# Sums, low halves and splits of two inner norms and an output projection on one engine, with the norms' partition sums moved in the matmul order

## The chip, the cores and the metric

The kernel runs on one core of one Trainium2 chip. The core has five engines that run side by side, each working through its own instructions in order: TensorE (PE, matrix products), VectorE (DVE), ScalarE (ACT), GpSimd (POOL) and SyncE (SP, which here issues transfers). The metric is the device time of one execution in microseconds (us). Before the change the median of 3 runs is 2609.95 us (2608.35 to 2614.61).

## The reference

The program computes one layer of a hybrid decoder for a prompt of 1024 tokens and 8 single tokens of other sequences (the sample group), 1032 tokens in all, with model width 1024 and float32 throughout:

```python
x = layer_norm(ALPHA * x + 0.5 * swiglu(x, ffn1_w1, ffn1_w3, ffn1_w2), ln1_g, ln1_b)
m, st = hybrid_mixer(x, h0, rc0, S0, gc0, w_in, b_in, ...)
x = layer_norm(ALPHA * x + m, ln2_g, ln2_b)
x = layer_norm(ALPHA * x + 0.5 * swiglu(x, ffn2_w1, ffn2_w3, ffn2_w2), ln3_g, ln3_b)
```

swiglu(x, w1, w3, w2) is (silu(x w1) * (x w3)) w2 with an inner width of 2816. layer_norm takes the mean of each token over its 1024 values, subtracts it, takes the mean of the squares, multiplies by the reciprocal root of that, then by a weight, and adds a bias. The mixer projects x (w_in), runs a gated linear recurrence and a gated delta rule with 8 heads, gates and adds both, and multiplies the merged result by w_o.

## The kernel before

**Layout.** Activations lie with the model width on the 128 partitions, as 8 blocks (KD = 8), and the tokens along the row, in 3 chunks of 344 (TC). ACC holds the running values. TensorE takes its operands in a reduced form (fp32r), so every float32 value that goes into a product is split: a high half (h, a copy made by ScalarE) and a low half (l, value minus high half, made by DVE or POOL). `split` (L87) makes both, and `mm3_steps` (L124, matmul at L132) makes each product of three: h with xh, h with xl, l with xh. For the activations the halves are XH and XL; for weights wh and wl; for the last group of the down projections both are called w2h; for the merged input of the output projection their buffers bear names such as m_pre, m_lt, m_ga. A weight block comes as wraw (128 x 512) by a transfer of SyncE and is split in the same manner. `tt` (L91) is a two-operand operation on DVE or, if told so, on POOL, and `stt` (L94) one of DVE with two operations in one. In the profile they bear these two lines, wherever they are called from.

**Norms.** The class `LN` is a norm of one chunk in four steps. `add` adds the blocks of the chunk up as they are finished (tile s, from the tag s1; POOL for all but the last block). The first step of `finish` multiplies this sum by a matrix of ones on TensorE (L176; this is the sum of values over the partitions, and its mean is mu), subtracts the mean from the 8 blocks (DVE), squares them (ScalarE, tile lnq), and adds the squares in two partial sums, one on DVE and one on POOL. The second step is again a product with ones at L176, the sum of squares, then logarithm and exponential on ScalarE (tile rs) for the reciprocal root. The third applies it: a DVE operation with weight and root (ACC<-ACC,LNT,mu), bias and high half on ScalarE (XH), low half (XL) on DVE for blocks 0, 2, 4, 6 and on POOL for blocks 1, 3, 5, 7 (ON_POOL). Norm 2 also writes its output to the DRAM tile X2 from POOL's queue.

Norm 1 follows the first feed-forward, norm 2 the mixer, norm 3 the second feed-forward (4 chunks of 258 tokens, the last, the tail, by a way of its own).

**Who calls the steps.** `last_steps` (L507) runs the units of the projection ahead of a norm (one block of output for one chunk, 24 matmuls for the output projection, 12 for the last group of a down projection), and puts the norm of chunk t between the units of chunk t+1: its first step after unit 0, the second and third after unit LN_STEP = 4 (5 for norm 3). The norm of the last chunk is handed on to the next stage, as `fin`: `kqv_first` (L685) for norm 1, and the start of the second feed-forward (`plain`, L361) for norm 2.

**What sets the order.** The code writes down the order of issue, but a scheduler of the framework then orders each engine's instructions, except where a pin keeps them in program order. Within an engine, the order so made is kept. The output projection (w_o; `msplit` L1119, `unit` L1125) runs while the last head of the delta rule and the sample group's branch (`sample`, L1180) finish; `sample` yields to the main stream `wait(n)` times n between its small products, so a higher n puts its next product later among the matmuls.

Of the kernel before, what the change touches and what calls it, by code (L numbers as in the profile page):

```python
# [44 lines left out]
LAST = 0.97  # L45
LN_STEP = 4
WO_RATE = 2.53
SIDE = 2
ON_POOL = (1, 3, 5, 7)

# [6 lines left out]
def _build(ctx, tc, A):  # L57
# [97 lines left out]
    class LN:  # L155
# [5 lines left out]
        def add(self, m):  # L161
            y = ACC[:, m, self.s]
            self.order.append(m)
            self.ys.append(y)
            n = len(self.ys)
            if n == 2:
                self.s1 = third("s1", self.w)
                tt(self.s1, self.ys[0], y, OP.add, G)
            elif 2 < n < (KD - 1 if self.tail else KD):
                tt(self.s1, self.s1, y, OP.add, G)  # L170
            elif n == KD and not self.tail:
                tt(self.s1, self.s1, y, OP.add, V)

# [4 lines left out]
        def finish(self):  # L178
# [10 lines left out]
            for k in (0, 1, 3, 2, 4, 6, 5, 7) if self.tail else range(KD):  # L189
                y = ys[k]  # L190
                if not self.tail:
                    tt(y, y, mu, OP.subtract)
                elif k in (2, 5):
                    tt(y, y, mu, OP.subtract, G)
                else:
                    stt(y, pm, -1.0 / D, y, OP.mult, OP.add)
                q[k] = third("s2" if k < 2 else "s1" if self.tail and k > 5 else "lnq", w)
                act(q[k], y, AF.Square)
                if self.tail:
                    if k in (1, 2, 6, 7):  # L200
                        tt(q[k], q[k], q[{1: 0, 2: 3, 6: 4, 7: 5}[k]], OP.add)
                        parts.append(q[k])
                elif k > 1:
                    tt(q[k % 2], q[k % 2], q[k], OP.add, (V, G)[k % 2])
            if not self.tail:
# [4 lines left out]
            self.total(pv, parts)  # L210
            rs = third("mu", w)
            act(rs, pv, AF.Ln, scale=1.0 / D, bias=EPS)
            exps.append(act(rs, rs, AF.Exp, scale=-0.5))
            yield
            for i, (k, y) in enumerate(zip(self.order, self.ys)):
# [11 lines left out]
                h, l = XH[:, k, self.s], XL[:, k, self.s]  # L227
                if i in ON_POOL or self.gi == 2:
                    act(y, y, AF.Identity, bias=b_)
                    split(h, l, y, G if i in ON_POOL else V)  # L230
                    if self.gi == 2:
                        G.dma_start(X2[:, k, self.s], y)
                    continue
# [113 lines left out]
    def ffn(n, lnidx, out=None, side=None, fin=None):  # L347
# [16 lines left out]
        def plain(f, put, after=None, w=None, chunks=range(NT), raws=None):  # L364
            a1, a3 = w or weights(f, raws=raws)
            for t in chunks:
                s = ts(t)
                if n == 1 and f == 0 and t:
                    x_load(t)
                    x_split(t)  # L370
                p1 = psum("mm")
                mm3(p1[:, :TC], a1, xsl(t), KD)
                if fin and f == 0 and t < 2:
                    for _ in range(1 + t):
                        next(fin)
                p3 = psum("g")
                mm3(p3[:, :TC], a3, xsl(t), KD)
                put(s, p1[:, :TC], p3[:, :TC])
                if after:
                    after(t)  # L380
                if n == 1:
                    next(extra, None)
# [45 lines left out]
        with pool("ffnb%d" % n) as up:  # L428
# [26 lines left out]
            for gi, fs in enumerate(GROUPS):  # L455
# [25 lines left out]
                else:  # L481
# [6 lines left out]
                    def last(m, t, s, i):  # L488
                        if t == 0:
                            held[m] = w2load(m, eng=(V, G)[m % 2], hold=hold if n == 2 or m < 6 else None)  # L490
                        unit(m, t, s, held[m])
# [15 lines left out]
    def last_steps(lnidx, unit, chunks, order, out=None):  # L507
        fin = None
        for t, s in enumerate(chunks):
            tail = out is not None and t == len(chunks) - 1  # L510
            ln = LN(lnidx, s, out, tail)
            for i, m in enumerate(order[t]):
                yield from unit(m, t, s, i) or ()
                ln.add(m)
                if fin and i == 0:
                    next(fin)
                if fin and i == LN_STEP + (out is not None):
                    next(fin)
# [10 lines left out]
    def mixer(mc):  # L529
# [74 lines left out]
        with pool("mix") as mp:  # L604
# [80 lines left out]
            def kqv_first():  # L685
# [16 lines left out]
                next(fin)  # L702
                kq(0, 1)
                kq(1, 0)
                next(fin)
                next(fin)
                kq(1, 1)
                kq(0, 2)
                kq(1, 2)
# [408 lines left out]
            def msplit(t):  # L1118
# [3 lines left out]
                for k in range(KD):  # L1122
                    h, l = MHL[t][2 * k:2 * k + 2]
                    split(h[:, :n], l[:, :n], ACC[:, k, t * TC:t * TC + n], (V, G)[k % 2])

# [3 lines left out]
            def unit(m, t, s, i):  # L1129
                ms = MHL[t]  # L1130
                if i > 1 or t == 0:
                    if len(recent) == 2:
                        recent.pop(next(iter(recent)))
                    recent[m] = wload(A["w_o"][m], KD, eng=(V, G)[m % 2])
                p = psum("mm" if (m + t) % 2 else "g")
# [48 lines left out]
    def sample(c, up, tk, ta, blk, half):  # L1184
# [40 lines left out]
        nc.scalar.dma_start(A["conv_new"], SPX)  # L1225
        yield from wait(12)
        pn = psum("sq")
# [5 lines left out]
        V.tensor_scalar(DG, IDT, rn[:, 1:], None, op0=OP.mult)  # L1233
        yield from wait(6)
        nc.scalar.dma_start(A["s_h"], H0)
# [10 lines left out]
        V.tensor_copy(KE[:, 0], K_)  # L1246
        yield from wait(6)
        pq = psum("sq")
# [25 lines left out]
        tt(M, OS, OS, OP.mult)  # L1274
        yield from wait(8)
        pn = psum("sq")
# [9 lines left out]
        nc.scalar.dma_start(RTD, rt)  # L1286
        yield from wait(6)
        pn = psum("sq")
# [131 lines left out]
```

## Time and profile before

| | us |
|---|---|
| median of 3 runs (2608.35 to 2614.61) | 2609.95 |
| the profiled execution's own time | 2612.26 |
| its span | 2610.5 |
| busy TensorE (PE) | 2532.2 (97%) |
| busy DVE | 1742.9 (67%) |
| busy ScalarE (ACT) | 1134.0 (43%) |
| busy POOL | 467.4 (18%) |

The profile is of one execution, taken on the chip; its granted clock of TensorE is 0.986 of full speed in the mean. A row of a group reads: line, engine, operation, output tile<-input tiles, count | busy us and mean ns of one | idle time of the engine before it, and what ended that. A row of the waits reads: engine, what waited, then the engine and tile that it waited for: us in total, times, longest. A row of a timeline starts with start and duration in us. Shares of busy time are means over the whole span.

### The profile page before, as it was taken

The numbers are of one execution on the slowest core, as the hardware profiler recorded it, in microseconds if no ns is written. First come the engines' busy times: TensorE is split into PE (matmuls) and PEld (weight loads), VectorE is DVE, ScalarE is ACT, GpSimd is POOL, SyncE is SP. The second block draws the span as 40 slices with busy tenths as digits, with TensorE's granted clock in tenths as the row PEclk, the third lists the DMA queues.
The fourth block names the chain that finished last, engine by engine and source line by source line (L and its number), as shares of the span: only waits on it lengthen the run. The fifth ranks groups of instructions, "written<-read, shape, count | busy, mean of one in ns | idle before, by whom it ended". The sixth has DMA issues, their size and how long they took to land.

```text
span 2610.5 us, 47260 instructions
## 1 busy us (share of the span) xinstructions
PE 2532.2 (97%) x18374; PEld 2485.7 (95%) x18374; DVE 1742.9 (67%) x3641; ACT 1134.0 (43%) x2426; POOL 467.4 (18%) x633
## 2 busy tenths in 40 slices
PE   9999999999999999999999999998799999999996
PEld 8999999999888999999999999988799999999996
DVE  7666665644696676777767686777766666656446
ACT  5323333221463736565564637635533333332125
POOL 2000000300432112111112121134521111121013
PEclk9999999999998999999999999999899999999998
DMA  6222222432101111111111111124453444333221
GB/s 228 82 76 83 79 79 75 116 98 86 46 30 47 36 49 45 38 50 36 54 37 53 34 57 37 47 89 132 124 154 102 120 123 111 102 117 111 82 69 66
DMA packets 151135, 208.65 MB, mean 80 GB/s; under 512 B 35632, under 2 KB 76080, under 8 KB 150912
## 3 DMA queue, kind: packets, MB, share of 16 engines
q1 hardware_dynamic: 126176, 156.24, 19.6%
q0 software_dynamic: 13904, 43.34, 6.0%
q10 hardware_dynamic: 10832, 6.07, 0.8%
q8 instruction: 144, 2.36, 0.4%
q14 instruction: 79, 0.65, 0.1%
HBM read 164.60 MB, written 40.99 MB: 79 GB/s over the span
## 4 chain that ended last, share of the span: by engine, by line
PE 83%; ACT 6%; DVE 6%; DMA 1%; issue 1%; POOL 1%; ACTq 0%; SPq 0%; DVEq 0%; POOLq 0%
PE ps_mm L132 34%; PE ps_g L132 13%; PE ps_g L298 10%; PE ps_mm L298 10%; PE ps_sq L298 8%; PE ps_g L892 2%; ACT L88 2%; DVE ACC L94 2%; PE ps_sq L778 2%; ACT lnq L88 1%; PE ps_g L778 1%; PE ps_g L784 1%; DVE ACC L91 1%; POOL s L91 1%; DVE wl L91 1%
## 5 line engine op out<-in xcount | busy, mean ns | idle before, releaser
L132 PE MATMUL ps_mm<-XH,wh 128*128 128x344 f32 x1656 | 558.3, 337 | 6.1 <-ACT wh L88 5.8
L132 PE MATMUL ps_mm<-XH,wl 128*128 128x344 f32 x1656 | 532.9, 322 | 0.0
L132 PE MATMUL ps_mm<-XL,wh 128*128 128x344 f32 x1656 | 532.6, 322 | 0.1
L88 ACT ACTIVATE wh<-wraw 128x512 fp32r<-128x512 f32 (+2 forms) x360 | 213.9, 598 | 408.8 <-PE ps_mm L132 140.9
L132 PEld LDWEIGHTS ps_mm<-XH,wh 128*128 128x128 f32 x1656 | 314.4, 190 | 9.6 <-ACT wh L88 5.8
L132 PEld LDWEIGHTS ps_mm<-XL,wh 128*128 128x128 f32 x1656 | 314.4, 190 | 1.8 <-DVE XL L91 0.6
L132 PEld LDWEIGHTS ps_mm<-XH,wl 128*128 128x128 f32 x1656 | 313.8, 190 | 0.4 <-DVE wl L91 0.2
L91 DVE TENSOR_TENSOR wl<-wraw,wh 128x512 fp32r<-128x512 f32 (+3 forms) x339 | 232.3, 688 | 42.5 <-ACT wh L88 38.4
L298 PE MATMUL ps_g<-CH,wh 128*128 128x258 f32 x740 | 209.0, 282 | 0.0
L298 PE MATMUL ps_g<-CH,wl 128*128 128x258 f32 x740 | 208.9, 282 | 0.0
L298 PE MATMUL ps_g<-CL,wh 128*128 128x258 f32 x740 | 208.7, 282 | 0.0
L88 ACT ACTIVATE wh<-S 128x512 fp32r<-128x512 f32 x148 | 93.4, 631 | 197.9 <-PE ps_sq L298 126.8
L298 PE MATMUL ps_mm<-XH,wh 128*128 128x258 f32 x592 | 167.2, 282 | 0.0
L298 PE MATMUL ps_mm<-XH,wl 128*128 128x258 f32 x592 | 166.9, 282 | 0.0
L298 PE MATMUL ps_mm<-XL,wh 128*128 128x258 f32 x592 | 166.8, 282 | 0.0
L353 POOL DMA_DIRECT2D gs<-G x74 | 40.5, 547 | 652.1 <-DVE G L91 604.2
L91 DVE TENSOR_TENSOR wl<-S,wh 128x512 fp32r<-128x512 f32 x148 | 102.3, 691 | 70.9 <-ACT wh L88 70.6
L88 ACT ACT_TABLE_LOAD x109 | 139.8, 1283 | 5.4 <-issue 2.6
L132 PE MATMUL ps_g<-gl,wh 128*128 128x344 f32 x444 | 142.2, 320 | 0.0
L132 PE MATMUL ps_mm<-gl,wh 128*128 128x344 f32 x444 | 142.0, 320 | 0.0
L132 PE MATMUL ps_g<-gh,wh 128*128 128x344 f32 x444 | 142.0, 320 | 0.0
L132 PE MATMUL ps_mm<-gh,wh 128*128 128x344 f32 x444 | 142.0, 320 | 0.0
(536 smaller groups left out, 6884.9 us busy)
## 6 DMA issues: line engine op xcount, KB each, us to landing
wraw<-w SPq DMA_DIRECT2D x164, 256.0 KB, 2.8
wraw<-w_in SPq DMA_DIRECT2D x128, 256.0 KB, 2.6
gr<-gs SPq DMA_DIRECT2D x84, 258.0 KB, 2.8
wr<-w SPq DMA_DIRECT2D x76, 256.0 KB, 2.6
gs<-G POOLq DMA_DIRECT2D x74, 258.0 KB, 2.6
wraw<-w_o SPq DMA_DIRECT2D x40, 256.0 KB, 2.8
x<-ACC POOLq DMA_DIRECT2D x24, 172.0 KB, 2.2
y<-ACC SPq DMA_DIRECT2D x32, 129.0 KB, 1.9
```

Of the source, the lines that this page charges most:

```text
L88: return S.activation(out, in_, f, **kw)
L91: return (eng or V).tensor_tensor(out, a, b, op=op)
L94: return V.scalar_tensor_tensor(out, a, s, b, op0=op0, op1=op1)
L132: PE.matmul(p, a, b, start=(n == 0), stop=(n == 3 * nk - 1))
L298: PE.matmul(ps_[c], a[:, k, :], b, start=(start and n == 0), stop=(n == 11), skip_group_check=not start)
L353: G.dma_start(gs[f][:, s], x)
L778: x = PE.matmul(ck(p, i), a, b, start=True, stop=True)
L784: x = PE.transpose(ck(p, i), a, IDT)
L892: pin(PE.matmul(o[r, c, :], a(c), b(c), start=True, stop=True))
```

## The change

1. The running sums of values (`LN.add`) and both partial sums of squares run on DVE. The tail of norm 3 keeps the two subtractions and the two products on POOL that it has now.
2. The low halves XL of norms 1 and 2 are all made on DVE, with one form of code for all blocks: norm 1's blocks 1, 3, 5, 7 also lose an extra pass of ScalarE (Identity). The transfers to X2 stay on POOL's queue. The tile rs comes from the tag s1, and no longer from mu.
3. The low halves of the last group of the down projections (w2h), of w_o (wl) and of the merged input (m_...) are all made on DVE.
4. The steps of the norms move: in `last_steps` the first step stands after unit 1 instead of 0, second and third after unit 6 instead of 4 (5 for norm 3). For the last chunk of norm 1, `kq(0, 2)` stands ahead of the second step. For that of norm 2 the second and third step come in the second weight group's first chunk and no longer in the first group's second. The waits of `sample` become 16, 14, 14, 16 and 14.

```diff
-LN_STEP = 4
+LN_STEP = 6
-ON_POOL = (1, 3, 5, 7)
...
             if n == 2:
                 self.s1 = third("s1", self.w)
-                tt(self.s1, self.ys[0], y, OP.add, G)
-            elif 2 < n < (KD - 1 if self.tail else KD):
-                tt(self.s1, self.s1, y, OP.add, G)
-            elif n == KD and not self.tail:
-                tt(self.s1, self.s1, y, OP.add, V)
+                tt(self.s1, self.ys[0], y, OP.add)
+            elif 2 < n < (KD - 1 if self.tail else KD + 1):
+                tt(self.s1, self.s1, y, OP.add)
...
                 elif k > 1:
-                    tt(q[k % 2], q[k % 2], q[k], OP.add, (V, G)[k % 2])
+                    tt(q[k % 2], q[k % 2], q[k], OP.add)
...
-            rs = third("mu", w)
+            rs = third("mu" if self.tail else "s1", w)
...
-                if i in ON_POOL or self.gi == 2:
+                if self.gi == 2:
                     act(y, y, AF.Identity, bias=b_)
-                    split(h, l, y, G if i in ON_POOL else V)
-                    if self.gi == 2:
-                        G.dma_start(X2[:, k, self.s], y)
+                    split(h, l, y)
+                    G.dma_start(X2[:, k, self.s], y)
                     continue
...
-                if fin and f == 0 and t < 2:
-                    for _ in range(1 + t):
+                if fin and t == 0 and f < 2:
+                    for _ in range(1 + f):
                         next(fin)
...
-                            held[m] = w2load(m, eng=(V, G)[m % 2], hold=hold if n == 2 or m < 6 else None)
+                            held[m] = w2load(m, hold=hold if n == 2 or m < 6 else None)
...
-                if fin and i == 0:
+                if fin and i == 1:
                     next(fin)
-                if fin and i == LN_STEP + (out is not None):
+                if fin and i == LN_STEP:
...
                 kq(0, 1)
+                kq(0, 2)
                 kq(1, 0)
                 next(fin)
                 next(fin)
                 kq(1, 1)
-                kq(0, 2)
...
-                    split(h[:, :n], l[:, :n], ACC[:, k, t * TC:t * TC + n], (V, G)[k % 2])
+                    split(h[:, :n], l[:, :n], ACC[:, k, t * TC:t * TC + n])
...
-                    recent[m] = wload(A["w_o"][m], KD, eng=(V, G)[m % 2])
+                    recent[m] = wload(A["w_o"][m], KD)
...
-        yield from wait(12)
+        yield from wait(16)
...
-        yield from wait(6)
+        yield from wait(14)
...
-        yield from wait(6)
+        yield from wait(14)
...
-        yield from wait(8)
+        yield from wait(16)
...
-        yield from wait(6)
+        yield from wait(14)
```

The instructions of the engines then stand in another order. Three places show it. The code after the change is 4 lines shorter: L176 is L173 in it, L132 is L131, L91 is L90 and L94 is L93.

The first is TensorE in the output projection, first of before, around the sample group's product with ones (L1238, tile St); the other rows are products of the merged input (m_...) of two blocks.

```order
L132 MATMUL ps_mm<-m_hLT,wh 128x344
L132 MATMUL ps_mm<-m_lt,wl 128x344
L132 MATMUL ps_g<-m_pre,wh 128x344 x2
L132 MATMUL ps_g<-m_pre,wl 128x344
L1238 MATMUL ps_sq<-St,ONES 128x128
L132 MATMUL ps_g<-m_pre,wh 128x344 x2
L132 MATMUL ps_g<-m_pre,wl 128x344
L132 MATMUL ps_g<-m_rR,wh 128x344
```

The same engine and place, of the kernel with the change.

```order
L131 MATMUL ps_mm<-m_v,wh 128x344 x2
L131 MATMUL ps_mm<-m_v,wl 128x344
L1234 MATMUL ps_sq<-St,ONES 128x128
L131 MATMUL ps_mm<-m_lt,wh 128x344 x2
L131 MATMUL ps_mm<-m_lt,wl 128x344
L131 MATMUL ps_mm<-m_lt,wh 128x344
```

St stood a few matmuls into a block (behind the second pair of its first operands, m_pre); it now stands late in the next block, behind its products of m_v. Between it and the sample group's product before it (L1228, now L1224, tile at), from which its chain starts, there are now 42 matmuls of the projection instead of 18.

The second place is TensorE at the start of the second feed-forward, around the sum of squares of chunk 2 of norm 2, first of before (tile s_20892; ps_mm and ps_g are the two accumulators, XH and XL the operands of the chunk).

```order
L132 MATMUL ps_mm<-XH,wh 128x344
L132 MATMUL ps_mm<-XL,wh 128x344
L132 MATMUL ps_mm<-XH,wl 128x344
L176 MATMUL ps_sq<-s_20892,ONES 128x344
L132 MATMUL ps_g<-XH,wh 128x344
```

And of the kernel with the change (tile s_20880; w1wr is a weight of the second group).

```order
L131 MATMUL ps_mm<-XL,w1wr 128x344
L131 MATMUL ps_mm<-XH,w1wr 128x344
L173 MATMUL ps_sq<-s_20880,ONES 128x344
L131 MATMUL ps_g<-XH,w1wr 128x344
L131 MATMUL ps_g<-XL,w1wr 128x344
```

It stood among the products of the first weight group and now stands among those of the second.

The third place is DVE in the first feed-forward's last group, at the squares of chunk 0 of norm 1, first of before (s_7806 and s_7809 are the two partial sums of squares; POOL adds the squares to s_7809).

```order
L91 TENSOR_TENSOR ACC<-ACC,mu 128x344 x5
L91 TENSOR_TENSOR s_7806<-s_7806,lnq 128x344
L91 TENSOR_TENSOR ACC<-ACC,mu 128x344 x2
L94 SCALAR_TENSOR_TENSOR ACC<-ps_g,ACC 128x344
L91 TENSOR_TENSOR s_7806<-s_7806,lnq 128x344
L94 SCALAR_TENSOR_TENSOR ACC<-ps_mm,ACC 128x344
L91 TENSOR_TENSOR s_7806<-s_7806,s_7809 128x344
L94 SCALAR_TENSOR_TENSOR ACC<-ps_g,ACC 128x344
```

And with the change (s_7822 and s_7825 are the partial sums, s_7814 the sum of values of chunk 1).

```order
L90 TENSOR_TENSOR ACC<-ACC,mu 128x344 x3
L90 TENSOR_TENSOR s_7825<-s_7825,lnq 128x344
L90 TENSOR_TENSOR s_7822<-s_7822,lnq 128x344
L90 TENSOR_TENSOR s_7825<-s_7825,lnq 128x344
L93 SCALAR_TENSOR_TENSOR ACC<-ps_mm,ACC 128x344
L90 TENSOR_TENSOR s_7822<-s_7822,s_7825 128x344
L90 TENSOR_TENSOR s_7814<-s_7814,ACC 128x344
L93 SCALAR_TENSOR_TENSOR ACC<-ps_g,ACC 128x344
```

Both partial sums and the next chunk's sum of values now stand in DVE's own order, and POOL's order has none of them.

## The prediction

> **What bounds the kernel now.** I read the page first, for its engine shares and its chain.
>
> ```profile
> PE 2532.2 (97%) x18374; PEld 2485.7 (95%) x18374; DVE 1742.9 (67%) x3641; ACT 1134.0 (43%) x2426; POOL 467.4 (18%) x633
> ...
> PE 83%; ACT 6%; DVE 6%; DMA 1%; issue 1%; POOL 1%; ACTq 0%; SPq 0%; DVEq 0%; POOLq 0%
> ...
> L88 ACT ACT_TABLE_LOAD x109 | 139.8, 1283 | 5.4 <-issue 2.6
> ```
>
> TensorE (PE) is busy for 2532.2 of the 2610.5 us of the span and carries 83% of the chain (the last row, ScalarE's table loads at 1.28 us, is used further down). The change takes no matmul away, so all it can win is in the 2610.5 - 2532.2 = 78.3 us in which TensorE stands, and in what a lowered clock adds to its busy time. The next view is the list of TensorE's waits; its columns are the total, the number of waits and the longest, in us.
>
> ```profile
> PE ps_sq L176 <- DVE s L91: 28.7, 12, 7.6
> ...
> PE ps_g L132 <- DVE wl L91: 4.8, 3, 4.1
> PE ps_sq L1238 <- DVE St L1233: 4.3, 1, 4.3
> ...
> PE ps_sq L1277 <- DVE kt L91: 1.9, 1, 1.9
> PE ps_mm L132 <- POOL wl L91: 1.9, 2, 1.6
> PE ps_mm L132 <- DVE m_lt L91: 1.6, 1, 1.6
> ```
>
> These six rows hold 43.2 us, over half of the idle time. The first is the norms: their partition sums (L176) stand in TensorE's order before the vector engine (DVE) has their input. The view of line L176, asked for each norm's stretch by itself (660 to 760, 1770 to 1900, 2530 to 2611 us), divides it.
>
> ```profile
>   DVE s L91: 7.6, 4
> ```
> ```profile
>   DVE s L91: 10.9, 3
> ```
> ```profile
>   DVE s L91: 10.2, 5
> ```
>
> So norm 1 has 7.6 us, norm 2 10.9 and norm 3 10.2. Then the table by stretch: the two ends, length and busy PE, PEld, DVE, ACT and POOL, then the granted clock (PEclk).
>
> ```profile
> 660.00:760.00 100.00, 88.63 (x518) 82.48 (x517) 82.17 (x139) 57.52 (x105) 47.43 (x47) 0.97 0.13 38
> 1700.00:1760.00 60.00, 54.39 (x338) 51.61 (x337) 41.83 (x87) 21.53 (x55) 23.87 (x23) 0.94 0.28 88
> 1810.00:1860.00 50.00, 38.05 (x196) 35.14 (x195) 40.76 (x59) 25.96 (x53) 33.27 (x37) 0.86 0.35 116
> 1860.00:1900.00 40.00, 32.22 (x182) 30.98 (x181) 23.70 (x42) 24.03 (x44) 21.48 (x27) 0.87 0.47 136
> 2560.00:2600.00 40.00, 30.35 (x192) 27.70 (x190) 28.25 (x70) 25.05 (x54) 13.93 (x19) 0.88 0.22 73
> ```
>
> The second norm and the output projection (1700 to 1900) are worst: in 1810 to 1860 TensorE works 38.05 of 50 us, at a clock of 0.86, while DVE is busy for 40.76. A mean of 67% hides that. The timeline of TensorE shows what a long wait costs besides itself (start, duration, idle time before it in brackets).
>
> ```profile
> 743.34 1.13 PE L176 MATMUL ps_sq<-s,ONES 128*128 128x344 f32 x2 [2.46 <-DVE s L91]
> ...
> 744.55 0.49 PE L132 MATMUL ps_mm<-XL,wh 128*128 128x344 f32 x1
> 744.84 0.49 PE L132 MATMUL ps_mm<-XH,wl 128*128 128x344 f32 x1
> ...
> 1746.57 0.48 PE L132 MATMUL ps_g<-m_pre,wh 128*128 128x344 f32 x2
> 1746.89 0.32 PE L132 MATMUL ps_g<-m_pre,wl 128*128 128x344 f32 x1
> 1751.47 0.80 PE L1238 MATMUL ps_sq<-St,ONES 128*128 128x128 f32 x2 [4.26 <-DVE St L1233]
> ...
> 1752.63 0.49 PE L132 MATMUL ps_g<-m_pre,wl 128*128 128x344 f32 x1
> 1752.92 0.49 PE L132 MATMUL ps_g<-m_rR,wh 128*128 128x344 f32 x1
> ...
> 1881.13 1.51 PE L176 MATMUL ps_sq<-s,ONES 128*128 128x344 f32 x2 [7.59 <-DVE s L91]
> ```
>
> Two matmuls start within 0.32 us before the wait of 4.26 (0.16 us each) and 0.29 us apart behind it. Each matmul at that pace loses 0.13 us, and some 17 of them 2.2 us. The row at 743.34 shows the same 0.29 us behind a gap of only 2.46 us. [...] I go by the row and charge any wait over 2.4 us about 2 us more.
>
> **Why DVE is late.** Two timelines, DVE's and then POOL's (GpSimd's), around 1841 and 1873 us.
>
> ```profile
> 1841.01 3.78 DVE L94 SCALAR_TENSOR_TENSOR ACC<-ACC,LNT,mu 128x344 f32<-128x344 f32 x1
> ...
> 1872.04 0.69 DVE L91 TENSOR_TENSOR w1S<-wraw,w1wr 128x512 fp32r<-128x512 f32 x1 [5.44 <-ACT w1wr L88]
> 1872.65 2.22 DVE L91 TENSOR_TENSOR ACC<-ACC,mu 128x344 f32<-128x344 f32 x5
> ```
> ```profile
> 1841.35 0.94 POOL L91 TENSOR_TENSOR XL<-ACC,XH 128x344 fp32r<-128x344 f32 x1
> 1842.23 0.94 POOL L91 TENSOR_TENSOR s<-s,ACC 128x344 f32<-128x344 f32 x1
> 1843.11 1.30 POOL L91 TENSOR_TENSOR wl<-wraw,wh 128x512 fp32r<-128x512 f32 x1
> ...
> 1875.05 5.45 POOL L91 TENSOR_TENSOR s<-s,lnq 128x344 f32<-128x344 f32 x3 [10.59 <-ACT lnq L88]
> ```
>
> Undisturbed, five DVE operations of 128x344 take 2.22 us, 0.44 each (one alone I take at 0.50, an estimate, since the ends of neighbours overlap), and one of 128x512 0.69. The one at 1841.01 took 3.78 us, while three POOL operations ran back to back from 1841.35 to 1844.41. It ended at 1844.79, behind the last of them. DVE's operation appears to have stood for all three. How far that holds on the whole is seen in the groups, kept apart by form, of 1690 to 1900 us (busy us, mean ns), of DVE and of POOL.
>
> ```profile
> L91 DVE TENSOR_TENSOR wl<-wraw,wh 128x512 fp32r<-128x512 f32 x26 | 23.7, 914 | 5.6 <-ACT wh L88 5.6
> L94 DVE SCALAR_TENSOR_TENSOR ACC<-ACC,LNT,mu 128x344 f32<-128x344 f32 x24 | 20.1, 886 | 3.8 <-ACT mu L88 3.8
> L91 DVE TENSOR_TENSOR ACC<-ACC,XL 128x344 f32<-128x344 f32 x24 | 16.8, 702 | 0.2
> ```
> ```profile
> L91 POOL TENSOR_TENSOR wl<-wraw,wh 128x512 fp32r<-128x512 f32 x20 | 27.6, 1384 | 11.1 <-ACT wh L88 9.2 <-ACT r L88 1.9
> L91 POOL TENSOR_TENSOR s<-s,ACC 128x344 f32<-128x344 f32 x15 | 15.0, 997 | 27.0 <-DVE ACC L91 18.3 <-DVE m_pre L91 3.5 <-PE ps_mm L132 3.5
> ...
> L91 POOL TENSOR_TENSOR s<-s,lnq 128x344 f32<-128x344 f32 x9 | 12.6, 1404 | 22.9 <-ACT lnq L88 22.5
> L91 POOL TENSOR_TENSOR XL<-ACC,XH 128x344 fp32r<-128x344 f32 x12 | 12.2, 1013 | 0.2
> ```
>
> **The change part by part.**
>
> *Moving work to DVE, norm 2 and output projection.* It takes over 20 weight splits, 20 x 0.69 = 13.8 us, and 15 + 9 + 12 small ones from the POOL rows, with 3 first sums and about 12 merged-input splits from the diff: 51 x 0.44 = 22.4. Together 36 us. What it gets back, if POOL no longer holds it: wl 26 x (0.914 - 0.69) = 5.8, LNT 24 x (0.886 - 0.50) = 9.3, the third row 24 x 0.20 = 4.8, together 19.9, and more from the groups not shown. Net, DVE has some 0 to 16 us more in a stretch of 210; it was not full in the mean, though it was locally. What POOL took 1.0 to 1.4 us for arrives after 0.44 to 0.69.
>
> *Norm 1.* The diff moves 18 sums, 9 adds of squares and 12 low halves (39 x 0.44 = 17.2) and 4 weight splits (2.8): 20 us on a DVE that is busy 82.17 of 100. The refund by the same rule lies between 0 and all of it.
>
> *Norm 3.* 23 sums, 9 adds, 4 splits: about 32 x 0.42 + 2.8 = 16 us, beside 28.25 of 40 busy; it fits. ScalarE loses 12 Identity passes in norm 1. I cost that at nothing, because ScalarE is at 57.52 of 100 there.
>
> *The later partition sums*, from the order of TensorE's instructions, at 0.16 us a matmul of 344 columns and about 0.12 at 258 (an estimate: 0.16 x 258/344). In norm 2 the sum of squares of chunk 1 stands 119 matmuls behind the sum of values instead of 41, 12.5 us later; that of chunk 2 80 instead of 49, 5 us later. The 10.9 us of that row are the 7.59 and 3.3 more. The 3.3 go. Of 7.59, 5.0 are covered by the shift, and the three POOL adds that took 5.45 us become three of 0.44, taking some 2 more: about 0.6 stays. With it goes the clock loss, 2.2. The sample group's norm (St, L1238) stands 42 matmuls behind the product that its chain starts from, instead of 18: 3.8 us more, against a wait of 4.26; the chain also sheds some of what POOL's operations add to it, so I let the wait go, with its 2.2 of clock. The wait on kt (1.9) goes too. Of the 4.8 on wl, 1.9 on POOL's wl and 1.6 on m_lt, 8.3 in all, DVE's strict order may keep half: I take 4, with bounds 0 and 8.3. Gains: 3.3 + 7.0 + 2.2 + 4.3 + 2.2 + 1.9 + 4 = 24.9.
>
> *What is late next.* Chunk 1's sum of squares now stands only 51 matmuls (8 us) ahead of the feed-forward's first matmul that reads that chunk. Behind it come the reciprocal root on ScalarE (about 3 us, an estimate from two table loads at 1.28 each) and 16 DVE operations of 0.44 = 7.0, of which TensorE needs the last only 21 matmuls after the first. So 3 + 7 + 2 of foreign work = 12 against 8 + 3.4: some 1 us of waiting, and up to 6 if DVE is behind; I take 2 and 2 for the clock. Chunk 2 has 73 matmuls, 11.7 us, and I take 1. Another 1 for residual waits elsewhere. Norm 2 gains 24.9 - 6 = 19; bounds 8 and 32.
>
> *Norm 1, sums.* Chunk 0's sum of squares moves 24 matmuls later, chunk 1's 20 (3 us each), chunk 2's 3. The waits of the first two (half of the 7.6) go. But chunk 2's sum of values comes 8 matmuls earlier behind an apply that is now all on DVE, and I expect several us there. I take 3.5 gained, bounds -3 and 9.
>
> *Norm 3, sums.* Chunk 1's moves 25 matmuls (3 us) later, chunk 2's 14 (1.7), against waits of about 2.4 each; the tail's 4.8 stays. The application of chunk 2 then runs beside the tail's squares on DVE, which gives back up to 2. I take 3.5, bounds -1 and 7.
>
> Sum: 19 + 3.5 + 3.5 = 26. The profiled execution took 2612.26 us, 1.76 more than its span and 2.31 above the median of 2609.95. 2612.26 - 26 = 2586.3; from the median **2584 us**.
>
> **The rivals.** A measurement of this kernel tells some 0.3%, 7.8 us, from no change.
>
> (a) *DVE becomes the local bound, and the waits only move.* In 1810 to 1860 it is at 40.76 of 50. If the refund is half, St, kt and one clock loss go (8.4) and chunk 2's later sum saves 5; norms 1 and 3 give nothing, and the first uses in the feed-forward cost 6 with 2 of clock: net 5, about 2605. For it: the two stretches at 82%. Against: the 3.78 us row. [...] The trace agrees that DVE is fullest where TensorE waits most, but no stretch quoted is full. Chance 0.15.
>
> (b) *DVE's long rows are not POOL's doing* (they would be waits inside the operation). Then there is no refund at all. DVE in 1810 to 1860 would need 40.76 plus some 16 of the 36 us, 57 in 50, 7 over; norm 1 has 82.17 + 20 = 102 in 100, and since its load is uneven I price 9 over, with two clock losses of 2; St, kt and one clock loss still go, -8.4. Net +12, about 2622. It decides from the point where under a third of the refund arrives. The row at 1841 speaks against it, and a POOL wl at 1.38 us is itself slow beside 1.30. Chance 0.08.
>
> (c) *Nearly all waits go.* The 43.2 us of the six rows, less the tail's 4.8, plus some 8 of clock, is 46: 2564. The 1810 to 1860 stretch, at a clock of 0.86, speaks for it, the new first-use waits against. Chance 0.07.
>
> (d) *The moves do not reach the queue*, since a scheduler orders it. The order shows them; chance 0.
>
> **How the numbers follow.** My forecast has 0.70, with its own range 2572 to 2600 from the bounds above taken partly together. The range to hold 8 in 10 reaches to (a): 2567 to 2608. Faster by over 7.8 us (under 2602): 0.66 of the forecast's 0.70, 0.07 of (c), 0.04 of (a), 0.77. Slower (over 2618): 0.06 of (b) and 0.02 of the forecast's and (a)'s edge, 0.08. Within: 0.15.
>
> **What would show it.** Right: the DVE group LNT at about 500 ns and wl at 690 ns in 1690 to 1900; no row for St L1238 and kt L1277 in TensorE's waits; L176's row near 10 us in place of 28.7, most of it norm 1's chunk 2 and the tail; a PEclk over 0.95 in the stretch of the output projection. Wrong: those two groups stay near 900 ns (b), or new rows of TensorE waiting for XL, XH or wl add up to over 15 us (a).

## The result and the profile after

The changed kernel takes 2580.66 us in the median of 4 runs (2576.32 to 2590.41), the kernel before 2610.55 in the 4 runs beside it (2608.35 to 2614.61): 29.9 us less, a ratio of 0.9889 with a 95% interval of 0.9858 to 0.992. The forecast was 26 us less, 2584. The sum came out nearly right; the experiments below show that much of its working was not.

The page of the changed kernel first, the rows of span and busy time.

```profile
span 2578.6 us, 47134 instructions
...
PE 2518.5 (98%) x18374; PEld 2475.0 (96%) x18374; DVE 1748.2 (68%) x3791; ACT 1126.3 (44%) x2414; POOL 310.4 (12%) x483
```

The span is 31.9 us shorter. TensorE's idle time fell from 78.3 to 60.1 us, and its busy time from 2532.2 to 2518.5 for the same 18374 matmuls: 18.2 us less of waiting and 13.7 less of busy time, which goes with the mean granted clock of 0.992 instead of 0.986. DVE took over 150 instructions (3641 to 3791), and its busy time rose by only 5.3 us, while POOL's fell by 157. TensorE's waits (us, times, longest), where they answer to the rows of before:

```profile
PE ps_sq L173 <- DVE s L90: 9.0, 6, 3.7
PE ps_g L131 <- DVE wl L90: 7.4, 3, 4.5
...
PE ps_mm L131 <- DVE ACC L93: 5.3, 1, 5.3
...
PE ps_mm L131 <- ACT XH L87: 2.2, 1, 2.2
```

The norms' sums wait 9.0 us instead of 28.7; the rows for St and for the second kt are gone. New are one wait of 5.3 us on an accumulator and one of 2.2 on XH, and the wait on wl has grown from 4.8 to 7.4. The same stretches as before in the table (the fourth falls on later work, since all comes earlier now):

```profile
660.00:760.00 100.00, 92.71 (x558) 86.51 (x557) 90.18 (x192) 55.56 (x101) 1.30 (x5) 0.97 0.13 41
1700.00:1760.00 60.00, 57.26 (x368) 56.02 (x367) 44.32 (x108) 24.27 (x57) 3.97 (x5) 0.94 0.33 106
1810.00:1860.00 50.00, 43.08 (x256) 41.72 (x255) 40.06 (x81) 28.04 (x56) 5.81 (x10) 0.97 0.45 134
1860.00:1900.00 40.00, 38.80 (x246) 38.31 (x245) 26.39 (x52) 24.20 (x43) 17.03 (x31) 1.00 0.69 216
```

In 1810 to 1860 TensorE now works 43.08 of 50 us at a clock of 0.97, instead of 38.05 at 0.86. DVE is fuller than before in norm 1, 90.18 of 100. The groups of DVE in 1690 to 1890 us (busy us, mean ns of one) say what became of its long operations:

```profile
L90 DVE TENSOR_TENSOR wl<-wraw,wh 128x512 fp32r<-128x512 f32 x47 | 32.0, 686 | 4.4 <-ACT wh L87 4.2
L93 DVE SCALAR_TENSOR_TENSOR ACC<-ACC,LNT,s 128x344 f32<-128x344 f32 x24 | 12.4, 572 | 5.1 <-ACT s L87 5.1
L90 DVE TENSOR_TENSOR ACC<-ACC,XL 128x344 f32<-128x344 f32 x24 | 12.2, 510 | 0.1
L90 DVE TENSOR_TENSOR XL<-ACC,XH 128x344 fp32r<-128x344 f32 x24 | 11.2, 509 | 0.3 <-ACT XH L87 0.2
```

wl fell from 914 to 686 ns, the application (LNT) from 886 to 572, the third from 702 to 510. 47 splits now cost DVE 32.0 us, where 26 cost 23.7.

To see where the time went, every profile is cut at the same instructions. Two rows of before, from the views of the tiles w2h and gu, show how: the last part of a row gives the first and the last start.

```profile
L132 PE MATMUL ps_g<-gh,w2h x200: 277/285/781, 665.3 to 2590.4; 128*128 128x258 f32 x64, 128*128 128x344 f32 x36
```
```profile
L812 PE MATMUL ps_g<-gu,SLR x32: 390/394/507, 786.3 to 1633.0; 128*128 128x512 f32 x32
```

From the first product of w2h to the first of gu is norm 1 with what runs beside it: 786.3 - 665.3 = 121.0 us. "Untouched" goes on from there to the first product of v and kt in the delta rule, and holds none of the changed code; "norm 2" from the last product of v and kt to the last of w1S (output projection, norm 2, first weights of the second feed-forward); "ffn 2" to the last product of CH; "norm 3" to the last of w2h; "tail" to the end of the span. One profiled execution each, us:

| kernel | norm 1 | untouched | norm 2 | ffn 2 | norm 3 | tail |
|---|---|---|---|---|---|---|
| before | 121.0 | 70.2 | 190.1 | 383.6 | 288.4 | 20.1 |
| after | 114.7 | 65.7 | 173.5 | 387.6 | 278.4 | 22.4 |
| parts 1 to 3 alone | 113.1 | 68.5 | 176.1 | 384.5 | 278.3 | 21.2 |
| part 4 alone | 122.4 | 69.0 | 179.5 | 386.2 | 287.5 | 22.1 |
| sample's waits alone | 121.0 | 70.5 | 192.0 | 384.6 | 288.0 | 20.4 |
| sums alone | 113.3 | 68.1 | 187.2 | 384.4 | 279.0 | 23.4 |
| splits alone | 118.1 | 67.3 | 184.3 | 384.6 | 287.1 | 20.0 |
| low halves alone | 116.8 | 69.8 | 182.5 | 384.3 | 288.9 | 20.3 |
| after, extra on POOL | 123.1 | 67.5 | 169.6 | 386.5 | 283.0 | 23.7 |
| after, extra on DVE | 119.5 | 65.0 | 180.5 | 387.1 | 280.0 | 25.8 |
| parts 1 to 3, norm 2's order | 113.1 | 68.5 | 178.2 | 384.5 | 278.5 | 20.9 |
| the same, and last sum later | 113.1 | 64.4 | 169.1 | 387.2 | 278.3 | 20.9 |
| all but the splits | 115.7 | 66.9 | 186.6 | 384.1 | 279.6 | 21.0 |
| after, tail on DVE too | 116.0 | 67.4 | 169.1 | 385.5 | 279.1 | 22.3 |

The change gains 6.3 us in norm 1, 16.6 in norm 2, 10.0 in norm 3 and 4.5 in the untouched stretch, and loses 4.0 in the second feed-forward and 2.3 in the tail; the rest of the 31.9 lies in between. The rows are not exact to the microsecond: in the last kernel of the table TensorE executes norm 2 in the same order as in the kernel after, and it took 169.1 us there instead of 173.5. A difference of 4 us between two rows of norm 2 is therefore no result by itself.

### The profile page after: what moved, and what is told of

It is laid out like the page before. It is cut to its first block, busy times and chain, and to the rows that moved or that the text cites. A ratio compares the mean times of both kernels' runs of the same rounds, so it can differ in the third digit from the quotient of the medians.

```text
span 2578.6 us, 47134 instructions
## 1 busy us (share of the span) xinstructions
PE 2518.5 (98%) x18374; PEld 2475.0 (96%) x18374; DVE 1748.2 (68%) x3791; ACT 1126.3 (44%) x2414; POOL 310.4 (12%) x483
## 5 line engine op out<-in xcount | busy, mean ns | idle before, releaser
L131 PE MATMUL ps_mm<-XH,wh 128*128 128x344 f32 x1656 | 557.4, 337 | 13.2 <-ACT wh L87 5.7
L131 PE MATMUL ps_mm<-XH,wl 128*128 128x344 f32 x1656 | 532.6, 322 | 0.0
L131 PE MATMUL ps_mm<-XL,wh 128*128 128x344 f32 x1656 | 531.1, 321 | 0.0
L131 PEld LDWEIGHTS ps_mm<-XH,wh 128*128 128x128 f32 x1656 | 313.6, 189 | 17.6 <-ACT wh L87 5.7
L131 PEld LDWEIGHTS ps_mm<-XL,wh 128*128 128x128 f32 x1656 | 313.6, 189 | 1.5 <-DVE XL L90 0.6
L131 PEld LDWEIGHTS ps_mm<-XH,wl 128*128 128x128 f32 x1656 | 313.0, 189 | 0.6 <-DVE wl L90 0.5
L90 DVE TENSOR_TENSOR wl<-wraw,wh 128x512 fp32r<-128x512 f32 (+2 forms) x360 | 239.0, 667 | 34.7 <-ACT wh L87 30.3
L90 DVE TENSOR_TENSOR wl<-S,wh 128x512 fp32r<-128x512 f32 x148 | 102.3, 691 | 68.9 <-ACT wh L87 68.5
L131 PE MATMUL ps_g<-gh,wh 128*128 128x344 f32 x444 | 142.3, 320 | 0.0
L131 PE MATMUL ps_g<-gl,wh 128*128 128x344 f32 x444 | 142.1, 320 | 0.0
L131 PE MATMUL ps_mm<-gl,wh 128*128 128x344 f32 x444 | 142.1, 320 | 0.0
L131 PE MATMUL ps_mm<-gh,wh 128*128 128x344 f32 x444 | 142.0, 320 | 0.0
L131 PE MATMUL ps_mm<-gh,wl 128*128 128x344 f32 x444 | 141.9, 319 | 0.0
```

The costliest lines, as they stand in the source:

```text
L90: return (eng or V).tensor_tensor(out, a, b, op=op)
L131: PE.matmul(p, a, b, start=(n == 0), stop=(n == 3 * nk - 1))
```

## The experiments

My theory going in: the gain comes from both halves of the change, the move of POOL's work (which lets DVE run at its own pace) and the later sums (which give it time). The rivals: only the order counts; or the work moved onto DVE delays TensorE; or DVE's long operations never were POOL's doing.

**Parts 1 to 3 alone.** The kernel after, with part 4 taken back:

```diff
-LN_STEP = 6
+LN_STEP = 4
...
-                if fin and t == 0 and f < 2:
-                    for _ in range(1 + f):
+                if fin and f == 0 and t < 2:
+                    for _ in range(1 + t):
...
-                if fin and i == 1:
+                if fin and i == 0:
...
-        yield from wait(16)
+        yield from wait(12)
```

> Parts 1 to 3 of the change alone (all sums, low halves and splits on the vector engine); the code's order of the norms' steps, of kq(0, 2) and of the sample group's waits as before. Theory (the refund of the vector engine and the later partial sums each carry a part of the gain): the groups ACC<-ACC,LNT near 570 ns and wl near 690 ns in the output projection as after the change, but St (4.3 us with 2.2 of clock), kt (1.9) and part of the wait on the sums of squares stay: 8 us faster than before, 3 to 14. Rival 1 (only the order counts): within 3 us of before. Rival 2 (work moved onto the vector engine without later sums delays TensorE): 4 to 10 us slower.

Measured: 2582.1 us against 2611.18, ratio 0.9883 (0.9868 to 0.9899), 29.1 us faster: all of the change's gain, over twice what I had expected at most. Every theory is missed, mine by too little faith in the move. (The scheduler also ordered TensorE's work somewhat differently from before here, in about a tenth of the places of norm 2.) The wait on St, which I expected to stay, is gone, although St stands where it stood before, 18 matmuls of the projection behind the product at L1224:

```profile
1735.18 0.38 PE L1224 MATMUL ps_sq<-ONES,at 128*128 128x128 f32 x2
...
1738.24 0.38 PE L1234 MATMUL ps_sq<-St,ONES 128*128 128x128 f32 x2
```

St comes 3.0 us behind that product without any idle time, where it came 8.6 us behind with 4.26 of waiting. The wait on the second kt is gone, too. So the faster DVE ended these two waits here, with no later place in the order.

**Part 4 alone.** The kernel before, with the step numbers, kq(0, 2) and the waits of the change.

> Part 4 of the change alone (norm steps, kq(0, 2), the sample group's waits), with sums, low halves and splits on POOL and the vector engine as before. Theory: St and kt go, and the later sums of squares cover 3.3 + 5 + 2.2 us of norm 2 and some 3 to 6 in norms 1 and 3, but the vector engine's groups stay long (ACC<-ACC,LNT 800 to 900 ns, wl about 900 ns in the output projection) and the waits on wl remain: 15 us faster than before, 8 to 22. Rival 1 (only the order counts): 25 to 32 us faster, as the whole change. Rival 2 (without the vector engine's refund the later sums run into the first uses of the chunks): 0 to 6 us faster.

Measured: 2605.53 us, ratio 0.9978 (0.9969 to 0.9986), 5.7 us faster. The groups of DVE in 1690 to 1890 us stay long:

```profile
L91 DVE TENSOR_TENSOR wl<-wraw,wh 128x512 fp32r<-128x512 f32 x26 | 22.5, 867 | 9.7 <-ACT wh L88 9.7
L91 DVE TENSOR_TENSOR ACC<-ACC,XL 128x344 f32<-128x344 f32 x24 | 18.3, 764 | 0.3
...
L94 DVE SCALAR_TENSOR_TENSOR ACC<-ACC,LNT,mu 128x344 f32<-128x344 f32 x23 | 14.5, 685 | 4.9 <-ACT mu L88 4.9
```

Rival 2 has it: later sums without a faster DVE run into other waits. By the table norm 2 gains 10.6 us, and norm 1, the second feed-forward and the tail give 6 of it back (1.4, 2.6 and 2.0).

**The sample group's waits alone.** The kernel before with one edit, of five like it:

```diff
-        yield from wait(6)
+        yield from wait(14)
```

> The kernel before with nothing but the sample group's waits of part 4 (16, 14, 14, 16, 14). Theory: the rows St L1238 (4.3 us, with 2.2 of clock behind it) and kt L1277 (1.9) leave TensorE's waits: 8 us faster than before, 4 to 9. Rival (the time they fill is only taken over by the next wait, on wl or the sums of the second norm, since the vector engine is the one that is late there): within 3 us of before.

Measured: 2612.38 us, ratio 1.0007 (0.9995 to 1.0018): nothing. TensorE's waits show why.

```profile
PE ps_sq L176 <- DVE s L91: 27.7, 11, 6.6
PE ps_mm L132 <- ACT wh L88: 10.3, 2, 5.7
PE ps_mm L132 <- POOL wl L91: 6.9, 4, 4.4
```

The wait on St is gone and that on the second kt is down to 0.2 us, as they should be, and the wait on DVE's wl fell from 4.8 to 0.2. But the wait on POOL's wl went from 1.9 to 6.9, that on wh from 5.8 to 10.3, and within norm 2 the sums' wait from 10.9 to 12.6. From the first to the last matmul of that stretch TensorE was idle for 26.8 us before and for 26.4 now, so the time of the waits that ended went over to others: norm 2 took 192.0 us, not less than 190.1. The rival was right.

**Extra work on POOL.** The kernel after, with one line more:

```diff
             elif 2 < n < (KD - 1 if self.tail else KD + 1):
                 tt(self.s1, self.s1, y, OP.add)
+            if n > 1:
+                tt(XL[:, m, self.s], self.ys[0], y, OP.add, G)
```

> The kernel after the change, with 77 additions more on POOL: each time a block is added to a norm's sum, POOL also adds two blocks into a place that is not read before it is overwritten (7 per chunk, 128x344 or 128x258). TensorE's order is that of the kernel after, instruction for instruction; nothing waits for the results but the overwriting, microseconds later. Theory (POOL's additions hold up the vector engine's operations with two inputs from SBUF): each costs the vector engine up to its own 0.7 to 1.0 us; ACC<-ACC,mu, s<-s,ACC and ACC<-ACC,LNT grow from 0.51 to 0.57 us to a mean of 0.6 to 0.8 in the three norms, and the time grows by 3 to 12 us. Rival (POOL work that nobody waits for is free, and the old long operations had another cause): the groups stay at 0.51 to 0.57 us and the time within 2 us of the kernel after.

Measured: 2597.45 us (2586.77 to 2599.22), ratio to before 0.9937 (0.992 to 0.9954): 13.7 us of gain left of 29.9. TensorE executes the same order, and nothing needs what POOL computes. DVE's groups in 660 to 785 us with the extra work:

```profile
L93 DVE SCALAR_TENSOR_TENSOR ACC<-ACC,LNT,s 128x344 f32<-128x344 f32 x24 | 14.4, 633 | 0.0
L90 DVE TENSOR_TENSOR s<-s,ACC 128x344 f32<-128x344 f32 x18 | 13.9, 771 | 0.2
...
L93 DVE SCALAR_TENSOR_TENSOR ACC<-ps_mm,ACC 128x344 f32<-128x344 f32 x14 | 7.1, 505 | 1.4 <-PE ps_mm L131 1.4
```

And in the same stretch of the kernel after, without it:

```profile
L93 DVE SCALAR_TENSOR_TENSOR ACC<-ACC,LNT,s 128x344 f32<-128x344 f32 x24 | 12.8, 569 | 0.0
...
L90 DVE TENSOR_TENSOR s<-s,ACC 128x344 f32<-128x344 f32 x18 | 9.2, 508 | 0.2
...
L93 DVE SCALAR_TENSOR_TENSOR ACC<-ps_mm,ACC 128x344 f32<-128x344 f32 x14 | 7.1, 508 | 2.3 <-PE ps_mm L131 2.2
```

DVE's addition, which stands right beside POOL's, goes from 508 to 771 ns, and norm 1 from 114.7 to 123.1 us. Of these 18 additions the 16 that overlap an operation of POOL took 804 ns in the mean, the other two 504. That an operation of POOL holds DVE up is shown here, apart from any change of order. Norm 3 went from 278.4 to 283.0. Norm 2 shows no loss (169.6, where two profiles with the same order of TensorE have 173.5 and 169.1); what the extra work costs there is not shown.

**The same work on DVE.** The same line without `, G`.

> The kernel after the change with the same 77 additions more as in the run with extra work on POOL, but on the vector engine, each 0.42 (258 columns) to 0.51 us (344), 37 us in all. Theory (an addition on POOL holds the vector engine's two-input operations for up to its whole duration, so POOL saves the vector engine nothing): 8 to 20 us slower than after, about what the extra work on POOL costs (17 us). Rival (an addition on POOL still relieves the vector engine, it only disturbs it somewhat): 25 to 37 us slower, clearly more than on POOL.

Measured: 2599.61 us (2593.03 to 2607.25), ratio 0.9961 (0.9947 to 0.9975): 11.3 us of gain left, 18.6 lost, where the extra work on POOL lost 16.2. The intervals of the two overlap. 77 additions cost this kernel about the same on either engine, as the theory has it; by this POOL relieves DVE of little or nothing. (Here the scheduler ordered TensorE's work differently, most of all in norm 2, so the two are not equal in all else.)

**One part at a time.** The kernel before with only the sums on DVE (without `G` in `LN.add` and in the squares), with only the splits of weights and merged input (without `(V, G)[m % 2]` and `(V, G)[k % 2]`), and with only the low halves:

```diff
-                if i in ON_POOL or self.gi == 2:
+                if self.gi == 2:
...
-                    split(h, l, y, G if i in ON_POOL else V)
+                    split(h, l, y)
```

> The kernel before with only the running sums and both partial sums of squares on the vector engine (low halves, splits and order as before). POOL loses some 83 us of work in the three norms. Theory (the gain goes with the POOL time taken away beside a late vector engine): half of the 29 us that all three parts gave together, 15 us faster than before, 8 to 20. Rival (what is left on POOL, low halves and splits, still holds the vector engine, so that a part alone gives little): 0 to 6 us faster.

> The kernel before with only the low halves of the weights (last group of the down projections, output projection) and of the merged input on the vector engine. POOL loses some 50 us, nearly all in the output projection. Theory (in proportion): 9 us faster than before, 4 to 14. Rival (a weight's split that is queued behind the norms' work on the vector engine comes later than from POOL): 2 to 8 us slower.

> The kernel before with only the low halves XL of norms 1 and 2 on the vector engine (and, with them, norm 1's extra ScalarE pass gone). POOL loses 25 us. Theory (in proportion): 5 us faster than before, 1 to 9. Rival (part alone gives nothing): within 2 us of before.

Measured, all against 2610.88 us: sums 2594.34 us, ratio 0.9942 (0.993 to 0.9954), 16.5 faster; splits 2599.49, 0.9963 (0.9951 to 0.9976), 11.4 faster; low halves 2597.51, 0.9955 (0.9943 to 0.9966), 13.4 faster. Each pays alone; the rivals are out. Sums and splits come as expected by POOL's time, the low halves pay more than twice what I had given them (a pass of ScalarE goes with them, too; no run tells the two apart). The table says where: the sums in norms 1 and 3 (7.7 and 9.4), low halves and splits in norm 2 (7.6 and 5.8). The wait on St, in the same place of the order in all three, stays with the sums alone (3.6 us) and the low halves alone (4.3) and is gone with the splits alone: it was the splits on POOL that made St late (with all but the splits moved, the next experiment, it stays at 3.7).

**All but the splits.** Parts 1 to 3, with half of the splits on POOL again.

> Parts 1 to 3 without the splits: sums and the low halves of the norms on the vector engine, half of the splits of the weights and of the merged input on POOL as before, order as before. The three parts alone gave 16.5, 11.4 and 13.4 us, 41 together, where all at once gave 29. Theory (they overlap, the last one taken gives least): 4 to 11 us slower than all three parts, 2586 to 2593. Rival (splits are worth their full 11 us or more beside the others): 2593 or more.

Measured: 2590.97 us against 2608.7, ratio 0.9932 (0.9919 to 0.9944), 17.7 us faster. The time is in the theory's range, but set against each one's own before, 29.1 - 17.7 = 11.4 us are missing, what the splits gave alone. So by the medians the splits add up with the rest, and it is sums and low halves that overlap: 16.5 and 13.4 alone, 17.7 together. The intervals leave a few microseconds open on either side.

**A better order.** Parts 1 to 3, with the later steps only where they serve norm 2, and the sample group's waits:

```diff
-                if fin and i == 0:
+                if fin and i == (lnidx == 2):
...
-                if fin and i == LN_STEP + (out is not None):
+                if fin and i == (6 if lnidx == 2 else LN_STEP + (out is not None)):
```

> Parts 1 to 3 of the change, and of part 4 only what concerns the output projection and norm 2: the steps after units 1 and 6 there, and the sample group's waits. Norms 1 and 3, kq(0, 2) and the start of the second feed-forward keep the order before. Theory (the later order helps norm 2 by some 3 us and costs as much in the second feed-forward and norm 1): 3 us faster than the kernel after, about 2578. Rival (with the vector engine relieved, the order no longer matters): 2579 to 2583, as the kernel after and the run without part 4.

Measured: 2579.15 us (2575.05 to 2582.82), ratio 0.988 (0.9864 to 0.9895). The rival's range has it: no difference that I can tell from the kernel after. Then the same with the last sum of squares of norm 2 moved into the second weight group, as in the change:

> As the run just above, with the sum of squares of norm 2's last chunk moved into the second weight group as well, as the change has it. Theory: it takes the wait before that sum away (3.9 us without part 4, 1.2 after the change), but new waits of the second feed-forward's first weights and gated values (3 us) come with it: within 2 us of the run above. Rival: 3 us faster than it.

Measured: 2571.54 us (2570.03 to 2573.59), ratio 0.9856 (0.9843 to 0.987): 37.2 us faster than before, and each of its runs below every run of the kernel after. The rival is nearer, and more came of it than it said. The wait ahead of that sum went from 4.63 us to 0.76, and the first matmuls behind it, which started 0.29 us apart, now start 0.16 apart: norm 2 took 169.1 us instead of 178.2, the second feed-forward 387.2 instead of 384.5. Some 4 us of the difference in these two profiles lie in the untouched stretch (68.5 and 64.4), where TensorE's order is the same in both. Set beside the kernel after, this one has the same order of TensorE in norm 2, and before's order of the steps in norms 1 and 3. In norm 1 the wait of 5.3 us on the accumulator is gone, and TensorE is idle for 2.9 us instead of 7.3. So the later places of part 4 seem worth some 8 us in norm 2 once DVE is relieved (37.2 us faster than before against 29.1 for parts 1 to 3 alone; the intervals just touch), and its places in norm 1 cost time.

**The tail on DVE too.** The kernel after without the `G` of the tail's two subtractions and two products.

> The kernel after the change, with the tail's four operations that are left on POOL (two subtractions, two products, 0.75 us each on POOL) on the vector engine too, 0.42 each. Theory (beside a busy vector engine POOL's work gains nothing): 0 to 2 us faster than after. Rival (in the tail the vector engine is alone on the path, and POOL runs beside it): 1 to 3 us slower.

Measured: 2578.59 us (2573.15 to 2583.89), ratio 0.9883 (0.9868 to 0.9897), 30.1 us faster than before, as the kernel after. The tail took 22.3 us against 22.4. Nothing to gain there, nothing lost; four operations are too few to tell the theories apart.

## Why the prediction was right, and where it was not

**The mechanism that carried the sum** was right: DVE was late because POOL's operations held it up, and taking them over costs DVE little. The prediction had 0 to 16 us more work for DVE in norm 2. Its busy time in that stretch of the table fell from 135.4 to 123.8 us, with some 50 instructions more; over the whole span it rose by 5.3. One term was a little off: an undisturbed application takes 572 ns and not 500, so that group gave back 7.5 us and not 9.3. Rival (b), that the long operations are not POOL's doing, is refuted three times: by the groups after, by part 4 alone (still 867 and 685 ns), and by the extra work on POOL. The runs show that the operations of the two engines contend: DVE's addition took 508 ns in the kernel after and 771 with the extra work on POOL, and one application of DVE took 3.78 us before, while three operations of POOL ran back to back. By what means they contend is not shown.

**The signs** that the prediction named came out nearly as it had them. The application (572 ns) and wl (686) are short, the rows for St and the second kt are gone, and the sums wait 9.0 us. The clock was 0.94 in the first of the three stretches of the output projection and norm 2, and 0.97 and 1.00 in the others, where over 0.95 was asked. The waits on wl and XH are 11.3 us (7.4 and 2.2, and 1.7 on a wl of the second feed-forward), under the 15 of rival (a).

**The step that failed** is "The later partial sums, from the order of TensorE's instructions". In norm 2 it booked 4.3 + 2.2 + 1.9 us for St and kt, 3.3 + 5.0 for the sums and 2.2 of clock to the order, 18.9 of 24.9. Most of this came from DVE's speed. With parts 1 to 3 alone, and the norms' steps and the sample group's waits as before, the waits on St and kt are gone, and norm 2 with the second feed-forward gains 13.1 us. Alone, the sample group's waits gave nothing, and all of part 4 gave 5.7 us; beside parts 1 to 3 it gave 1.4 by the medians (2582.1 and 2580.66 in different sets), less than the intervals can tell from nothing; in norm 1 it cost time. A wait that ended was not worth its length while DVE was late with everything behind it: it handed its time to the next wait (with the sample group's waits alone TensorE was idle for 26.4 us in norm 2, where it had been 26.8). I had used this argument in rival (a) and not in the sum.

**Norm 2's size is not settled**: 19 was forecast, with the first uses in the second feed-forward counted in; 16.6 less 4.0 was measured, 12.6, inside the bounds of 8 and 32. The two kernels of the table that have the same order of TensorE in norm 2 and the second feed-forward, with no extra work, give 21.0 less 1.9 (tail on DVE too) and 21.0 less 3.6 (last sum later), 19.1 and 17.4. So the size may have been right, for another reason than the one given: over the 13.1 us of parts 1 to 3 alone, the later places add 6.0 and 4.3 in these two profiles, and nothing in that of the kernel after. The first use of chunk 1 waits 2.2 us, as taken (2); the last chunk's sum of squares 1.2 instead of 0.6. The wait on wl was to halve, and it grew. The timeline of DVE in the kernel after shows how:

```profile
1813.87 0.51 DVE L90 TENSOR_TENSOR s<-s,lnq 128x344 f32<-128x344 f32 x1
1814.30 0.51 DVE L90 TENSOR_TENSOR ACC<-ACC,mu 128x344 f32<-128x344 f32 x1
1814.80 1.37 DVE L90 TENSOR_TENSOR s<-s,lnq 128x344 f32<-128x344 f32 x3
1816.09 0.94 DVE L90 TENSOR_TENSOR ACC<-ACC,mu 128x344 f32<-128x344 f32 x2
1816.94 0.69 DVE L90 TENSOR_TENSOR wl<-wraw,wh 128x512 fp32r<-128x512 f32 x1
```

The high half of that block began on ScalarE at 1813.76 and took 0.63 us. The split waited behind five operations of the norm until 1816.94, and TensorE with it, 4.49 us. That is the strict order that the prediction named, mis-sized: it took 4 us gained on wl and m_lt, of 8.3; these waits came to 7.4 there, so the gain was 0.9.

**Norms 1 and 3 came out larger.** Norm 1: 3.5 forecast, 6.3 measured (7.9 without part 4). The several us that I expected at chunk 2 are there, at another instruction: DVE works through an application first, and the accumulator that TensorE needs is read behind it.

```profile
722.36 2.03 DVE L93 SCALAR_TENSOR_TENSOR XL<-ACC,LNT,XH 128x344 fp32r<-128x344 f32 x4
724.31 1.06 DVE L93 SCALAR_TENSOR_TENSOR ACC<-ACC,LNT,s 128x344 f32<-128x344 f32 x2
725.28 0.51 DVE L93 SCALAR_TENSOR_TENSOR ACC<-ps_mm,ACC 128x344 f32<-128x344 f32 x1
```
```profile
725.85 0.65 PE L131 MATMUL ps_mm<-XH,wh 128*128 128x344 f32 x1 [5.31 <-DVE ACC L93]
```

Norm 3: 3.5 forecast, 10.0 less 2.3 of the tail measured. I had costed the move there at nothing ("it fits") and given the gain to the order. The runs show the reverse: sums on DVE alone gain 9.4, part 4 alone 0.9.

**What no term held**: 4.5 us in the untouched stretch, which is not shown to be a gain of the change (the last section has the clocks there). Together, by the one profile of the kernel after: norm 2 was 6.4 too high, norm 1 2.8 and norm 3 4.2 too low, and 5 us came from elsewhere. The errors offset one another, and the total was good for less than good reasons: that it came so near is in part luck.

## What to carry to other kernels

Where VectorE is late and GpSimd runs two-input operations beside it, compare the mean of one VectorE form where GpSimd is busy and where it is not; if it differs, as here with 771 against 508 ns, bring the GpSimd work home first, and look at the order afterwards. Do not add up the waits of one late engine: until the engine itself is faster, a wait taken away may come back at a later instruction, as here, where the wait of 4.3 us on St ended and norm 2 kept 26.4 of 26.8 us of idle time. And after such a move look for the urgent short operation (a weight's split, the reading of an accumulator) that now stands behind a norm's long run of operations in the same queue (here 4.49 and 5.31 us of waiting).

## What the runs showed of the hardware

An operation of DVE that reads one operand from an accumulator (ACC<-ps_mm,ACC) was not held up by POOL: 505 ns with the extra work, 508 without, while the addition with both operands in SBUF (s<-s,ACC) went from 508 to 771. This is no accident of time: of the 27 operations that read ps_mm or ps_g in that stretch, 12 overlap an operation of POOL, and these took 504 ns in the mean, the others 507.

The granted clock of the untouched stretch differed between two executions whose TensorE does the same there in the same order, 0.88 before and 0.97 after:

```profile
786.30:856.50 70.20, 66.09 (x468) 62.99 (x469) 47.52 (x117) 24.86 (x69) 15.44 (x23) 0.88 0.16 43
```
```profile
779.70:845.40 65.70, 60.45 (x467) 57.06 (x468) 47.49 (x117) 24.61 (x69) 16.21 (x23) 0.97 0.17 47
```

The same wait shows it, first of before and then of after, with the rows behind it.

```profile
794.90 2.04 PE L778 MATMUL ps_g<-kq,kq 128*128 128x128 f32 x8 [1.92 <-DVE kt L91]
...
797.02 0.49 PE L132 MATMUL ps_mm<-XL,wh 128*128 128x344 f32 x1
797.31 0.49 PE L132 MATMUL ps_mm<-XH,wl 128*128 128x344 f32 x1
```
```profile
788.32 1.16 PE L774 MATMUL ps_g<-kq,kq 128*128 128x128 f32 x8 [1.92 <-DVE kt L90]
...
789.48 0.32 PE L131 MATMUL ps_mm<-XL,wh 128*128 128x344 f32 x1
789.64 0.32 PE L131 MATMUL ps_mm<-XH,wl 128*128 128x344 f32 x1
```

After the same 1.92 us the matmuls start 0.29 us apart in one execution and 0.16 in the other. So the length of a wait alone does not decide, and my charge of 2 us for each wait over 2.4 was too simple. What decides besides it is not shown. Over the kernels of the table the stretch took 64.4 to 70.5 us, and differences of 3 to 5 us between two profiles here are no result.
